# Differential attention's rotation and mixing: sums on GpSimd, coefficients for three tiles, another order of features

## The chip, the core and the metric

The kernel runs on one core of a Trainium2 chip. A core has five engines, each with its own stream of instructions, which it works through in order: TensorE (PE: matmuls, with weight loads shown apart as PEld), VectorE (DVE), ScalarE (ACT), GpSimd (POOL) and SyncE (SP, which here issues DMAs). They wait for each other through semaphores. SBUF and PSUM are the on-chip memories; PE writes to PSUM. The metric is the device time of one launch in microseconds; lower is better.

## The reference

Two post-norm layers, each a feed-forward half step, a token mixer, a cross-attention into 256 memory tokens, and a second feed-forward half step. Layer 0's mixer is the differential attention that this change touches; layer 1's is a pooling mixer. There are 512 tokens of 1024 features, all float32.

```python
q = rope(q.reshape(B, S, H, 2, dk), c5, s5)      # H = 8 heads, 2 components, dk = 64
k = rope(k.reshape(B, S, H, 2, dk), c5, s5)      # feature e is rotated with feature e + 32
lam = exp(sum(lq[0] * lk[0])) - exp(sum(lq[1] * lk[1])) + lam_init
s = einsum('bqhcd,bkhcd->bhcqk', qblk, k) * dk ** -0.5     # one score matrix per component
p = softmax(where(mask, s, min), axis=-1)
a = p[:, :, 0] - lam * p[:, :, 1]
o = einsum('bhqk,bkhe->bqhe', a, v)
o = o * rsqrt(mean(o ** 2) + eps) * subln_g * (1 - lam_init)
```

## The kernel before, in words

A float32 product is made of three matmuls: each operand is split into a high part (a cast, on ScalarE) and a low part (what the cast left out, a subtraction on VectorE), and high by high, low by high and high by low are summed in PSUM. `wh` and `wl` are the parts of weights, `qk` those of queries and keys, `a` those of mixed probabilities, `v` those of values.

`da_main` projects, head by head, query and key, and for every second head the values of two heads. `da_side` does the rest of a head: scores, softmax, mixing, the product with the values, the norm. `weave` writes the two into one program: after each piece of `da_main` it lets `da_side` go on, by estimated times, so that PE has projections to work on while a head's softmax runs on the other engines. A scheduler of the framework then fixes one order for each engine, and every engine keeps to its own at run time.

What the change and the prediction speak of, by the lines of the kernel before:

- `cols_rope` (L290, L293): splits one head's query or key weights, and puts the features of a head in an order that suits the rotation. The cast is one operation over 128 x 1024. The low part is two operations, one for each half of the features' quarters, over 128 x 512 each. There are 16 such weights.
- `da_rope` (L1129 to L1132): rotates a projected query or key. A shuffle on VectorE swaps the 16-partition halves of each group of 32 into `t2`; VectorE multiplies the projection by the cosines into `t1`; GpSimd multiplies `t2` by the sines; VectorE adds both. Then come the high part (ScalarE, L140 for a query, L135 for a key) and the low part (VectorE, L141 or L136). It runs 16 times.
- `da_scores` (L1162, L1171, L1174): PE's scores for the four tiles of 128 tokens, i = 0 to 3, tile i over the first (i + 1) x 128 keys and for both components. All six banks that PE and the other engines share here are taken for them, also the one into which the squares of the head before (L1220) are written. Then, on VectorE, mask and minimum (L1171), and on ScalarE the exponentials with their row sums (L1174).
- `da_mix` (L1187 to L1189): the reciprocal of the second component's row sum, the coefficient from it, and the mix, for one tile after another. It stands behind the masks of the head's last tile.
- `da_turn` (L506 with `pt<-ident,p`): PE transposes the mixed tile; `a` is its high and low part.
- `da_out` (L1210, L1211, L1216, L1217, L1220, then L1227 to L1230): PE's product with the values into `po`; for two tiles at a time a copy on ScalarE and a sum on VectorE into `o`; the squares on ScalarE; after the last tile four small operations on GpSimd that end with a power. `da_scale` uses the result.

The tiles `t1` and `t2` come from one pool of two buffers.

Of the kernel before, what the change touches and what calls it, by code (L numbers as in the profile page):

```python
# [9 lines left out]
F32 = mybir.dt.float32  # L10
# [3 lines left out]
ALU = mybir.AluOpType  # L14
# [3 lines left out]
P = 128  # L18
D = 1024
S = 512  # L20
NT = S // P
# [98 lines left out]
class Trunk:  # L120
# [163 lines left out]
    def cols_rope(self, raw, j, wait=False):  # L284

        nc = self.nc
        w = self.hl([P, 8, P])
        src = raw[:, j].rearrange("p k (m h q e) -> p (k m) q h e", m=2, h=2, q=2)
        hi, lo = (t.rearrange("p k (m q h e) -> p (k m) q h e", m=2, q=2, h=2) for t in w)
        nc.scalar.copy(hi, src)  # L290
        with self.tc.issue_after(self.turned[1].ins) if wait else nullcontext():
            for q in range(2):
                self.last_low = nc.vector.tensor_sub(  # L293
                    lo[:, :, q], src[:, :, q], hi[:, :, q].bitcast(F32)
                )
        return w

    def wide(self, raw):
# [827 lines left out]
    def da_rope(self, ps):  # L1126
        nc = self.nc
        t1, t2 = self.tmp("rt"), self.tmp("rt")
        nc.vector.stream_shuffle(t2, ps, [(i + 16) % 32 for i in range(32)])  # L1129
        nc.vector.tensor_tensor(t1, ps, self.ropeC, ALU.mult)  # L1130
        nc.gpsimd.tensor_tensor(t2, t2, self.ropeS, ALU.mult)
        nc.vector.tensor_tensor(t1, t1, t2, ALU.add)  # L1132
        return t1

    def da_query(self, ps):
# [11 lines left out]
    def da_scores(self, st, before):  # L1147

        nc = self.nc
        q, k, mm, terms = st["q"], st["k"], self.nc.tensor.matmul, ((0, 0), (1, 0), (0, 1))  # L1150
# [11 lines left out]
                    mm(banks[i][m], q[a][rows, qi], k[b][rows, kn], start=a == b, stop=b == 1)  # L1162
        for i in SC_ORDER:
            n = (i + 1) * P
            mx, rc, cf = self.small("mx"), self.small("rc", (P, 1)), self.small("cf", (P, 1))
            sm = st["sm"][:, i]
            p = [self.tmp("p")[:, :n] for m in range(2)]
            with self.tc.high_priority():
                for m in range(2):
# [10 lines left out]
            st["m", i] = p, sm, rc, cf  # L1180

    def da_mix(self, st, i):

        nc = self.nc
        p, sm, rc, cf = st.pop(("m", i))
        with self.tc.issue_after(st["masked"].ins):
            nc.vector.reciprocal(rc, sm[:, 1:2])  # L1187
            nc.vector.scalar_tensor_tensor(cf, sm[:, 0:1], self.nlam, rc, ALU.mult, ALU.mult)
            nc.vector.scalar_tensor_tensor(p[0], p[1], cf, p[0], ALU.mult, ALU.add)  # L1189
        st["p", i] = p[0]  # L1190

# [573 lines left out]
```

## Time and profile before

| what | value |
|---|---|
| device time, median of 3 runs | 1913.4 us (1912.26 to 1915.36) |
| span of the profiled execution | 1913.0 us, granted TensorE clock 0.999 |
| attention heads, as part of the span | about 355 to 560 us |
| PE busy in that stretch | 200.5 of 205.0 us |
| the rotation's sums on VectorE, L1132 | 16 of 682 ns, 10.9 us |
| the rotation's products on GpSimd, L1131 | 16 of 1289 ns, 20.6 us |
| low parts of query and key weights, L293 | 32 of 833 ns, 26.0 us |
| reciprocals and coefficients, L1187 and L1188 | 32 of 156 ns and 32 of 211 ns |

The span runs from the first to the last instruction of one execution that a profiler recorded; the device times are those of other executions, without it. In a row of the timeline stand the start in us from the span's begin, the duration in us, the engine, the line of the kernel, the operation, what it writes and reads, the sizes and a count. In brackets is the time for which the engine sat idle before, and what ended that. An instruction's record may overlap the next one's by some 0.08 us, since engines work in a pipeline. A row of waits gives the waiting engine and line, the one that it waited for, the sum in us, the number of times and the longest.

### The profile page before, as it was taken

The numbers are of one execution on the slowest core, as the hardware profiler recorded it, in microseconds if no ns is written. First come the engines' busy times: TensorE is split into PE (matmuls) and PEld (weight loads), VectorE is DVE, ScalarE is ACT, GpSimd is POOL, SyncE is SP. The second block draws the span as 40 slices with busy tenths as digits, with TensorE's granted clock in tenths as the row PEclk, the third lists the DMA queues.
The fourth block names the chain that finished last, engine by engine and source line by source line (L and its number), as shares of the span: only waits on it lengthen the run. The fifth ranks groups of instructions, "written<-read, shape, count | busy, mean of one in ns | idle before, by whom it ended". The sixth has DMA issues, their size and how long they took to land.

```text
span 1913.0 us, 32564 instructions
## 1 busy us (share of the span) xinstructions
PE 1894.9 (99%) x13136; PEld 1733.1 (91%) x13136; DVE 1550.6 (81%) x2250; ACT 1003.8 (52%) x1546; POOL 317.3 (17%) x274
## 2 busy tenths in 40 slices
PE   9999999999999999999999999999999999999998
PEld 8999998888878888999998999999899889999997
DVE  7888889888867558889888988898787568898886
ACT  6555554566645435645554655455455436555552
POOL 3112120111110001221220311212130012211210
PEclk9999999999999999999999999999999999999999
DMA  9978772323225327987785687878344438877861
GB/s 248 216 166 187 166 146 82 91 67 89 89 67 155 111 66 198 182 179 162 144 192 179 109 179 165 183 163 184 111 133 133 134 87 171 178 159 166 188 132 56
DMA packets 246743, 277.96 MB, mean 145 GB/s; under 512 B 8256, under 2 KB 212544, under 8 KB 246592
## 3 DMA queue, kind: packets, MB, share of 16 engines
q0 software_dynamic: 92928, 92.29, 31.5%
q1 hardware_dynamic: 153664, 183.59, 30.0%
q8 instruction: 103, 1.69, 0.4%
q14 instruction: 48, 0.39, 0.1%
HBM read 273.75 MB, written 2.10 MB: 144 GB/s over the span
## 4 chain that ended last, share of the span: by engine, by line
PE 85%; DVE 10%; ACT 2%; DMA 1%; issue 1%; POOL 1%; SPq 0%; DVEq 0%; ACTq 0%; POOLq 0%
PE x L221 7%; PE x L220 7%; PE x L222 7%; PE ps L220 4%; PE z L221 4%; PE z L220 4%; PE z L222 4%; PE ps L222 4%; PE ps L221 4%; PE px L222 2%; PE px L220 2%; PE px L221 2%; PE pt L506 2%; PE y L222 2%; PE x L757 2%; PE xq L222 2%
## 5 line engine op out<-in xcount | busy, mean ns | idle before, releaser
L725 POOL DMA_DIRECT2D ra<-in_ffn_w_in_dram x132 | 170.7, 1314 | 982.3 <-DVE wl L732 966.5
L730 ACT CAST wh<-ra 128x1024 fp32r<-128x1024 f32 x176 | 185.1, 1053 | 208.0 <-PE x L221 63.3
L732 DVE TENSOR_TENSOR wl<-ra,wh 128x1024 fp32r<-128x1024 f32 x176 | 214.4, 1223 | 66.5 <-ACT wh L730 66.1
L220 PE MATMUL x<-xe,wh 128*128 128x256 f32 x704 | 195.0, 277 | 0.0
L221 PE MATMUL x<-xe,wh 128*128 128x256 f32 x704 | 194.8, 277 | 0.0
L222 PE MATMUL x<-xe,wl 128*128 128x256 f32 x704 | 194.8, 277 | 0.0
L730 ACT CAST wh<-rc 128x1024 fp32r<-128x1024 f32 x132 | 139.0, 1053 | 102.4 <-PE x L221 41.6
L135 ACT CAST wh<-b 128x1024 fp32r<-128x1024 f32 x112 | 117.8, 1052 | 130.4 <-PE x L221 66.1
L732 DVE TENSOR_TENSOR wl<-rc,wh 128x1024 fp32r<-128x1024 f32 x132 | 160.3, 1222 | 25.5 <-ACT wh L730 25.5
L136 DVE TENSOR_TENSOR wl<-b,wh 128x1024 fp32r<-128x1024 f32 x112 | 136.9, 1222 | 41.0 <-ACT wh L135 41.0
L220 PE MATMUL x<-xh,wh 128*128 128x256 f32 x536 | 148.7, 277 | 0.0
L221 PE MATMUL x<-xl,wh 128*128 128x256 f32 x536 | 148.3, 277 | 0.0
L222 PE MATMUL x<-xh,wl 128*128 128x256 f32 x536 | 148.3, 277 | 0.0
L220 PEld LDWEIGHTS x<-xe,wh 128*128 128x128 f32 x704 | 132.4, 188 | 1.3
L221 PEld LDWEIGHTS x<-xe,wh 128*128 128x128 f32 x704 | 132.3, 188 | 1.3
L222 PEld LDWEIGHTS x<-xe,wl 128*128 128x128 f32 x704 | 132.2, 188 | 0.0
L136 DVE TENSOR_TENSOR wl<-raw,wh 128x1024 fp32r<-128x1024 f32 x64 | 82.4, 1296 | 41.1 <-ACT wh L135 40.5
L221 PEld LDWEIGHTS x<-xl,wh 128*128 128x128 f32 x536 | 100.8, 188 | 0.7
L220 PEld LDWEIGHTS x<-xh,wh 128*128 128x128 f32 x536 | 100.7, 188 | 0.7
L222 PEld LDWEIGHTS x<-xh,wl 128*128 128x128 f32 x536 | 100.6, 188 | 0.0
L135 ACT CAST wh<-raw 128x1024 fp32r<-128x1024 f32 x64 | 66.4, 1049 | 61.0 <-PE xq L221 19.1
L220 PE MATMUL z<-xe,wh 128*128 128x256 f32 x352 | 97.5, 277 | 0.0
(447 smaller groups left out, 6266.0 us busy)
## 6 DMA issues: line engine op xcount, KB each, us to landing
ra<-in_ffn_w_in_dram POOLq DMA_DIRECT2D x132, 512.0 KB, 7.0
rc<-in_ffn_w_in_dram SPq DMA_DIRECT2D x88, 512.0 KB, 5.8
b<-in_ffn_w_out_dram SPq DMA_DIRECT2D x76, 512.0 KB, 4.8
ra<-in_ffn_w_in_dram SPq DMA_DIRECT2D x44, 512.0 KB, 4.7
rc<-in_ffn_w_in_dram POOLq DMA_DIRECT2D x44, 512.0 KB, 7.8
raw<-in_xa_wkv_dram SPq DMA_DIRECT2D x16, 1024.0 KB, 5.4
raw<-in_da_w_qkv_dram SPq DMA_DIRECT2D x16, 512.0 KB, 5.2
raw<-in_xa_wq_dram SPq DMA_DIRECT2D x8, 1024.0 KB, 5.7
```

The source lines that it names most:

```text
L135: self.nc.scalar.copy(hi, src),
L136: self.nc.vector.tensor_sub(lo, src, hi.bitcast(F32)),
L220: self.first_mm = mm(out, w[0], x[0], start=start, stop=False, skip_group_check=again)
L221: mm(out, w[0], x[1], start=False, stop=False, skip_group_check=again)
L222: self.last_mm = mm(out, w[1], x[0], start=False, stop=stop, skip_group_check=again)
L506: self.turns = [self.nc.tensor.transpose(pt[:, j], b, self.ident) for j, b in enumerate(blocks)]
L725: nc.gpsimd.dma_start(t, source(*block), accum_op=ALU.add)
L730: hi = nc.scalar.copy(v[0], raw)
L732: lo = nc.vector.tensor_sub(v[1], raw, v[0].bitcast(F32))
L757: self.last_mm = nc.tensor.matmul(ps[:, j], v[i][:, k, j * P : (j + 1) * P], x[l][:, k], start=n == i == l == 0, stop=n == 7 and i == 1, s ...
```

## The change

It has three parts, all in the differential attention.

1. In `da_rope` the sum of `t1` and `t2` moves from VectorE to GpSimd, right behind GpSimd's product.
2. In `da_mix` the reciprocals and coefficients of tiles 0 to 2 are made by one operation each, over three columns, when tile 0 is mixed; tile 3 has its own.
3. In `cols_rope` the features of a component are paired by parity: feature 2r + q goes to place 32q + r, where before the places were made of runs of 16. Features e and e + 32 still come to lie 16 places apart in one group of 32, so the shuffle is the same, and the table of frequencies follows. The low part becomes one operation over 128 x 1024 that reads every second element, and so does the cast.

```diff
-    rope = np.stack([inv[quarter * 16 + e], np.where(half == 0, -1.0, 1.0)], axis=1).astype(np.float32)
+    rope = np.stack([inv[2 * e + quarter], np.where(half == 0, -1.0, 1.0)], axis=1).astype(np.float32)
...
-        src = raw[:, j].rearrange("p k (m h q e) -> p (k m) q h e", m=2, h=2, q=2)
-        hi, lo = (t.rearrange("p k (m q h e) -> p (k m) q h e", m=2, q=2, h=2) for t in w)
+        src = raw[:, j].rearrange("p k (m r q) -> p (k m) q r", m=2, q=2)
+        hi, lo = (t.rearrange("p k (m q r) -> p (k m) q r", m=2, q=2) for t in w)
         nc.scalar.copy(hi, src)
         with self.tc.issue_after(self.turned[1].ins) if wait else nullcontext():
-            for q in range(2):
-                self.last_low = nc.vector.tensor_sub(
-                    lo[:, :, q], src[:, :, q], hi[:, :, q].bitcast(F32)
-                )
+            self.last_low = nc.vector.tensor_sub(lo, src, hi.bitcast(F32))
...
         nc.gpsimd.tensor_tensor(t2, t2, self.ropeS, ALU.mult)
-        nc.vector.tensor_tensor(t1, t1, t2, ALU.add)
+        nc.gpsimd.tensor_tensor(t1, t1, t2, ALU.add)
...
-            mx, rc, cf = self.small("mx"), self.small("rc", (P, 1)), self.small("cf", (P, 1))
-            sm = st["sm"][:, i]
+            mx, sm = self.small("mx"), st["sm"][:, i]
...
-            nc.vector.reciprocal(rc, sm[:, 1:2])
-            nc.vector.scalar_tensor_tensor(cf, sm[:, 0:1], self.nlam, rc, ALU.mult, ALU.mult)
+            if i in (0, NT - 1):
+                n = slice(0, NT - 1) if i == 0 else slice(i, NT)
+                rc, st["cf"] = self.small("rc", (P, NT)), self.small("cf", (P, NT))
+                rc, cf, sm = rc[:, n], st["cf"][:, n], st["sm"][:, n]
+                nc.vector.reciprocal(rc, sm[:, :, 1])
+                nc.vector.scalar_tensor_tensor(cf, sm[:, :, 0], self.nlam, rc, ALU.mult, ALU.mult)
+            cf = st["cf"][:, i : i + 1]
             nc.vector.scalar_tensor_tensor(p[0], p[1], cf, p[0], ALU.mult, ALU.add)
```

The scheduler's orders change with it. Line numbers of the changed kernel are three lower in `da_rope`. On VectorE, from the product of head 2's query with the cosines to the shuffle of its key, before and now (`wl` here are low weights of values, `o` is the output's sum, `a` the low part of head 1's mixed tiles):

```order
L1130 TENSOR_TENSOR rt<-q,ropeC 128x512
L136 TENSOR_TENSOR wl<-raw,wh 128x1024
L136 TENSOR_TENSOR a<-pt,a 128x384
L1132 TENSOR_TENSOR rt<-rt 128x512
L1217 TENSOR_TENSOR o<-o,po 128x256
L141 SCALAR_TENSOR_TENSOR qk<-rt,qk 128x512
L136 TENSOR_TENSOR a<-pt,a 128x512
L1129 STREAM_SHUFFLE rt<-k 128x512
```

```order
L1127 TENSOR_TENSOR rt<-q,ropeC 128x512
L136 TENSOR_TENSOR wl<-raw,wh 128x1024
L136 TENSOR_TENSOR a<-pt,a 128x384
L141 SCALAR_TENSOR_TENSOR qk<-rt,qk 128x512
L1218 TENSOR_TENSOR o<-o,po 128x256
L136 TENSOR_TENSOR a<-pt,a 128x512
L1126 STREAM_SHUFFLE rt<-k 128x512
```

The sum is gone, and the query's low part now stands ahead of the output's sum and of a. On ScalarE the query's high part stands likewise ahead of the output's copy, the first square and the cast of a.

On GpSimd, from head 2's rotations (query, key) to that of head 3's query, before and now (`f` are the four small operations of head 1's norm, and the first two of head 2's):

```order
L1131 TENSOR_TENSOR rt<-rt,ropeS 128x512 x2
L1229 TENSOR_TENSOR f<-f,sq 128x4
L1230 TENSOR_TENSOR f<-f,mhalf 128x4
L1131 TENSOR_TENSOR rt<-rt,ropeS 128x512
L1227 TENSOR_SCALAR f<-sd 128x4
L1228 TENSOR_TENSOR f<-f,sd 128x4
```

```order
L1128 TENSOR_TENSOR rt<-rt,ropeS 128x512
L1129 TENSOR_TENSOR rt<-rt 128x512
L1128 TENSOR_TENSOR rt<-rt,ropeS 128x512
L1129 TENSOR_TENSOR rt<-rt 128x512
L1230 TENSOR_TENSOR f<-f,sq 128x4
L1231 TENSOR_TENSOR f<-f,mhalf 128x4
L1128 TENSOR_TENSOR rt<-rt,ropeS 128x512
L1129 TENSOR_TENSOR rt<-rt 128x512
L1228 TENSOR_SCALAR f<-sd 128x4
L1229 TENSOR_TENSOR f<-f,sd 128x4
```

Each product has its sum right behind it; the two rows of the norm stand, as before, ahead of head 3's product.

On VectorE, from the key's product with the cosines at head 2 to the masks of head 2 (`q` is head 3's query), before and now:

```order
L1130 TENSOR_TENSOR rt<-k,ropeC 128x512
L293 TENSOR_TENSOR wl<-raw,wh 128x16x32
L1132 TENSOR_TENSOR rt<-rt 128x512
L1217 TENSOR_TENSOR o<-o,po 128x256
L293 TENSOR_TENSOR wl<-raw,wh 128x16x32
L136 TENSOR_TENSOR qk<-rt,qk 128x512
L1129 STREAM_SHUFFLE rt<-q 128x512
L1130 TENSOR_TENSOR rt<-q,ropeC 128x512
L293 TENSOR_TENSOR wl<-raw,wh 128x16x32
L1132 TENSOR_TENSOR rt<-rt 128x512
L293 TENSOR_TENSOR wl<-raw,wh 128x16x32
L141 SCALAR_TENSOR_TENSOR qk<-rt,qk 128x512
```

```order
L1127 TENSOR_TENSOR rt<-k,ropeC 128x512
L292 TENSOR_TENSOR wl<-raw,wh 128x1024
L136 TENSOR_TENSOR qk<-rt,qk 128x512
L1218 TENSOR_TENSOR o<-o,po 128x256
L1126 STREAM_SHUFFLE rt<-q 128x512
L1127 TENSOR_TENSOR rt<-q,ropeC 128x512
L292 TENSOR_TENSOR wl<-raw,wh 128x1024
L141 SCALAR_TENSOR_TENSOR qk<-rt,qk 128x512
L1167 ISA p,mx<-sc,mask 128x128
```

The masks of head 2 stand behind the low part of head 3's query, before and now; the output's sum has come behind the key's low part.

More of the change, by code (lines that the diff above doesn't have):

```diff
@@ L1179, in da_scores @@
                         self.da_scale(before)
-            st["m", i] = p, sm, rc, cf
+            st["m", i] = p
     def da_mix(self, st, i):
         nc = self.nc
-        p, sm, rc, cf = st.pop(("m", i))
+        p = st.pop(("m", i))
         with self.tc.issue_after(st["masked"].ins):
-            nc.vector.reciprocal(rc, sm[:, 1:2])
-            nc.vector.scalar_tensor_tensor(cf, sm[:, 0:1], self.nlam, rc, ALU.mult, ALU.mult)
+            if i in (0, NT - 1):
[5 more added lines that the diff above has]
+            cf = st["cf"][:, i : i + 1]
             nc.vector.scalar_tensor_tensor(p[0], p[1], cf, p[0], ALU.mult, ALU.add)
```

## The prediction

> **What bounds the kernel now.** I read the page's busy shares first.
>
> ```profile
> PE 1894.9 (99%) x13136; PEld 1733.1 (91%) x13136; DVE 1550.6 (81%) x2250; ACT 1003.8 (52%) x1546; POOL 317.3 (17%) x274
> ```
>
> TensorE (PE) is busy 99% of the span, so an edit moves the end only by the time for which PE itself waits. The change touches the attention heads alone, from about 355 to 560 us; the table of waits for that stretch (first two lines) and for the rest (last line, PE's longest there) says what there is.
>
> ```profile
> PEld pt L506 <- DVE p L1189: 5.5, 5, 1.7
> PEld sc L1162 <- ACT po L1220: 0.9, 3, 0.4
> PE pk L222 <- DVE wl L136: 0.6, 2, 0.5
> ```
>
> Five times PE waits for a mixed tile before it transposes it (L506), 5.5 us in all: the most that the change can win. After 560 us PE hardly waits, so nothing there absorbs a shift: what the heads gain or lose reaches the end whole. Next, the timeline at the masks of head 2, where such a wait stands.
>
> ```profile
> 414.12 1.04 POOL L1230 TENSOR_TENSOR f<-f,mhalf 128x4 f32<-128x4 f32 x1
> 415.56 0.75 DVE L1129 STREAM_SHUFFLE rt<-q 128x512 f32<-128x512 f32 x1
> 416.38 1.29 POOL L1131 TENSOR_TENSOR rt<-rt,ropeS 128x512 f32<-128x512 f32 x1 [1.21 <-DVE rt L1129]
> 416.79 1.43 DVE L293 TENSOR_TENSOR wl<-raw,wh 128x512 fp32r<-128x512 f32 x1
> 418.14 0.68 DVE L1132 TENSOR_TENSOR rt<-rt 128x512 f32<-128x512 f32 x1
> 418.86 0.63 ACT L140 ACTIVATE qk<-rt 128x512 fp32r<-128x512 f32 x1 [2.49 <-DVE rt L1132]
> 419.52 0.69 DVE L141 SCALAR_TENSOR_TENSOR qk<-rt,qk 128x512 fp32r<-128x512 f32 x1
> 420.13 0.28 DVE L1171 CUSTOM_DVE_ANT_0 p<-sc,mask 128x128 f32<-128x128 f32 x1
> 423.42 0.30 DVE L1187 RECIPROCAL rc<-sd 128x1 f32<-128x1 f32 x3
> 423.88 0.74 DVE L1189 SCALAR_TENSOR_TENSOR p<-p,cf 128x128 f32<-128x128 f32 x2
> 424.28 0.33 PE L506 MATMUL pt<-ident,p 128*128 128x128 f32 x1 [0.87 <-DVE p L1189]
> ```
>
> This is head 3's query rotation, and head 2's masks (L1171) stand behind its last step (L141) on VectorE (DVE). So the rotation's length sets the masks of the head before, its mix, and PE's first transpose. That is the path to price.
>
> **Who has the port.** The L293 row took 1.43 us where the same row on an idle GpSimd (POOL) takes 0.68: it ended 0.55 us after GpSimd's product (416.38 + 1.29 = 417.67). What happens when both engines queue up shows in the pooling stage:
>
> ```profile
> 1397.81 1.29 POOL L1355 TENSOR_TENSOR X<-X,p 128x512 f32<-128x512 f32 x1 [4.94 <-DVE xl L136]
> 1407.90 2.06 DVE L136 TENSOR_TENSOR wl<-raw,wh 128x1024 fp32r<-128x1024 f32 x1 [0.18 <-ACT wh L135]
> 1408.85 2.26 POOL L1355 TENSOR_TENSOR X<-X,p 128x512 f32<-128x512 f32 x1
> 1409.89 2.30 DVE L136 TENSOR_TENSOR wl<-raw,wh 128x1024 fp32r<-128x1024 f32 x1
> 438.92 1.04 POOL L1230 TENSOR_TENSOR f<-f,mhalf 128x4 f32<-128x4 f32 x1
> 439.47 1.30 DVE L293 TENSOR_TENSOR wl<-raw,wh 128x512 fp32r<-128x512 f32 x2 [1.84 <-ACT wh L290]
> ```
>
> A GpSimd sum of this very shape (L1355) takes 1.29 alone. Behind another of its kind, with a VectorE operation of two SBUF inputs waiting (the low weights at 1407.90), it takes 2.26: VectorE gets the port between the two, and the next low operation waits in turn. They alternate. A low operation over 1024 ends 1.08 us after GpSimd lets go (1409.89 + 2.30 = 1412.19 against 1408.85 + 2.26 = 1411.11), and a sum that waited ends 1.14 us after the low operation (1411.11 against 1407.90 + 2.06 = 1409.96). The last two rows say that GpSimd's power over four columns does not hold VectorE up: two half operations in 1.30 beside it.
>
> **The change part by part.** *Coefficients.* Three reciprocals at 0.07 and the coefficients at 0.13 each stood before the first mix (423.42 to 423.88, 0.46); one of each over three columns makes about 0.33, as it waits for the third tile's exponentials, which the third reciprocal did too. So 0.13 earlier per head. Head 0's third tile is also mixed before the key's rotation.
>
> *Low weights.* One operation over 1024 in place of two over 512. Between the bounds 1.22 (contiguous, as 1.08 + 0.14 above) and twice that (each element of the read with step two costing two) I take 1.22: the old form, with broken runs, cost 0.65 per 512, like a contiguous row. By the Trainium skill (SBUF — State Buffer, the note on cachelines under Door 1: The DMA port swizzle) a step of up to four fp32 reads at full rate; that would give the same 1.22, and no row here reads with step two.
>
> *The sum.* From the end E of GpSimd's product, the sum was over at E + 1.15 (418.82): half a low operation, then 0.68. Now the whole low operation gets the port at E, ends at E + 1.08, and GpSimd's sum at E + 2.23: 1.07 later. If GpSimd kept the port it would end at E + 1.27, but the low operation at E + 2.35, and L141 stands behind it: 0.4 later instead. The rows above alternate, so I take 1.07. The 16 sums leave VectorE (16 of 0.68, 11 us), but that time lay beside PE's projections; where VectorE sat waiting before and after the sum is what counts.
>
> *What queues behind it.* ScalarE and VectorE now have L140 and L141 ahead of the output's copy, sum and squares, which used to go first. Head 2's query shows the price:
>
> ```profile
> 402.59 0.74 DVE L1129 STREAM_SHUFFLE rt<-q 128x512 f32<-128x512 f32 x1
> 404.47 1.32 DVE L136 TENSOR_TENSOR wl<-raw,wh 128x1024 fp32r<-128x1024 f32 x1
> 406.77 0.41 DVE L1217 TENSOR_TENSOR o<-o,po 128x256 f32<-128x256 f32 x1
> 406.88 0.63 ACT L140 ACTIVATE qk<-rt 128x512 fp32r<-128x512 f32 x1 [1.44 <-DVE rt L1132]
> 407.42 0.27 ACT L1220 ACTIVATE po<-o 128x128 f32<-128x128 f32 x1
> 407.71 0.57 ACT L135 CAST a<-pt 128x512 fp32r<-128x512 f32 x1
> 408.31 0.69 DVE L136 TENSOR_TENSOR a<-pt,a 128x512 fp32r<-128x512 f32 x1
> 409.66 0.22 PE L1211 MATMUL po<-v,a 128*128 128x128 f32 x1
> 413.37 0.28 ACT L1220 ACTIVATE po<-o 128x128 f32<-128x128 f32 x1
> 413.85 0.20 POOL L1229 TENSOR_TENSOR f<-f,sq 128x4 f32<-128x4 f32 x1 [2.62 <-ACT po L1220]
> ```
>
> GpSimd's sum ends at 405.79 + 1.14 = 406.93; L140 starts at 406.96, L141 0.67 later at 407.63, the output's sum at 408.23 (was 406.77), the square at 408.67, the cast of a at 408.96, its low part from 409.56 to 410.25. PE needs that at 409.66 and a weight load of 0.19 ahead: **0.8 us of new wait, head 1**.
>
> From there the key: shuffle at 410.17, product from 410.99 to 412.28, low operation to 413.36, sum to 414.50, L141 from 415.20, output's sum to 416.21, squares to 417.08 (was 413.77), then on GpSimd the f row and the power to 418.5. Head 3's query product stands behind these in GpSimd's queue, so it comes not at 416.38 but after 418.5; the low operation, whose cast was behind the squares, has the port from 418.08 to 419.22, the product ends at 420.44, the sum at 421.7, L141 at 422.4, the masks at 423.0 in place of 420.13. The transpose comes 2.85 - 0.13 = 2.7 us late, of which PE has waited 0.8: **1.9 more, head 2**. The same steps for head 4's query and key (its shuffle at 449.75, GpSimd's sum over at 454.1, L141 from 454.8, a's low part over at 457.4 and loaded by 457.6 against 456.73 below; then the squares at 464.2, the power to 465.6, masks 2.9 late) give **0.9 at head 3 and 1.9 at head 4**.
>
> The other places, with their rows:
>
> ```profile
> 377.54 0.33 PE L506 MATMUL pt<-ident,p 128*128 128x128 f32 x1 [0.21 <-DVE p L1189]
> 381.75 0.55 PE L506 MATMUL pt<-ident,p 128*128 128x128 f32 x3 [0.61 <-DVE p L1189]
> 384.73 0.60 PE L506 MATMUL pt<-ident,p 128*128 128x128 f32 x4
> 456.73 0.22 PE L1211 MATMUL po<-v,a 128*128 128x128 f32 x1
> 485.89 1.74 PEld L1162 LDWEIGHTS sc<-qk 64*128 64x128 f32 x24 [0.36 <-ACT po L1220]
> 492.06 1.29 POOL L1131 TENSOR_TENSOR rt<-rt,ropeS 128x512 f32<-128x512 f32 x1
> 494.66 0.33 PE L506 MATMUL pt<-ident,p 128*128 128x128 f32 x1 [1.26 <-DVE p L1189]
> 505.23 0.22 PE L1211 MATMUL po<-v,a 128*128 128x128 f32 x1
> 509.77 0.52 PEld L1162 LDWEIGHTS sc<-qk 64*128 64x128 f32 x5 [0.19 <-ACT po L1220]
> ```
>
> - Head 0: masks 1.4 late (1.07, and 0.3 from the key before it), less 0.13: +1.3 at 377.54. The wait at 381.75 goes, since the third mix no longer follows the key's rotation: -0.8. The fourth mix now stands behind the key's longer chain (sum at 383.9, L141 at 384.6, mix from 385.3 to 386.1) where PE wants it at 384.73 + 0.5: +0.9. Together **+1.4**.
> - Head 5: its scores wait for the squares, which move behind L141 by 0.6: **+0.6** at 485.89. Its mixes no longer wait for the key's sum, but they, and the coefficients, have two SBUF inputs and meet GpSimd's product (to 493.35) and sum (to 494.65): first transpose at about 495.2, **+0.5** at 494.66. If coefficients of three columns pass while GpSimd works, the first mix comes between product and sum, at 493.35, and PE waits at the second tile instead, for 0.2 less than now in all. The wide operations above all waited, so I take +0.5. By the Trainium skill (SBUF — State Buffer, SBUF: two separate sides) the lock is for every VectorE operation with two SBUF inputs against a GpSimd one that reads SBUF, which would give the same; no narrow one met GpSimd's wide product here.
> - Heads 5 and 6: the cast of a behind L140 as at head 1, low part at 506.4 against 505.23 + 0.5: **+0.8**. Then the key's chain ends with squares at 513.2 (were done by 509.72), and the scores that reuse their bank move from 509.77 to 513.3, 3.7 late with 1.35 paid: **+2.3**.
>
> Sum: 1.4 + 0.8 + 1.9 + 0.9 + 1.9 + 0.6 + 0.5 + 0.8 + 2.3 = 11.1 us on the span of 1913.0, that is 1924.1; the median of the runs lies 0.4 above that span, so **1924.5**. With the port kept by GpSimd the same walk gives +7.5, with every place a third dearer about +15: its own range is 1920 to 1929.
>
> **The rivals.** *The sum is hidden.* If GpSimd's sum ran right behind its product and the low operation cost nobody time, the chain would be 0.2 longer per query, the coefficients would pay 0.13 back, 0.8 and 1.0 of head 0's and 5's waits would go, and the new order would still cost some 0.5 at heads 1 and 3: 1912.5, no change. For it: GpSimd is 17% busy. Against it: the alternation at 1408.85. *VectorE relieved.* It loses 11 us of sums and some of the low and small operations. If all five waits at L506 came of VectorE's load, they would go: 1913.4 - 5.5 = 1908. Against it: at 415.56 to 420.13 VectorE stands in one chain, not in a backlog. It is decided by whether L141 starts earlier than E + 1.85. *Step two is dear.* If the low operation took 2.3 us, it would add 1.07 at some seven of the places above: 1932. For it: no row shows such a read.
>
> **How the numbers follow.** My forecast 0.68, hidden 0.14, relieved 0.09, dear 0.09. About 0.2% (3.8 us) is what a measurement of this kernel tells from no change, so the same is 1909.6 to 1917.2. Faster gets the relieved case and a little of the hidden one, 0.1; the same gets the rest of the hidden one and a tail of the forecast in which half the places have slack that I missed, 0.17; slower 0.73. The range from 1914 to 1931 leaves out 0.09 + 0.05 below and 0.06 above.
>
> **What would show it.** Right: low operations right behind GpSimd's product, and sums of about 2.2 us; the masks of heads 2 and 4 some 2.9 us later against PE's clock of matmuls; waits of PE at L506 that grow to 2 us and more; the power ahead of a late product. Wrong: sums of 1.3 us, L141 less than 2 us after E, or low operations well over 1.3 us on a free port.

## The result, and the profile after

The changed kernel took 1929.76 us in the median of four runs (1929.33 to 1930.07), the kernel before 1912.83 beside it: a ratio of 1.0089, with an interval of 1.0076 to 1.0102. It is slower by 16.9 us, on the side of the forecast. The time lies 5.3 us beyond the forecast's number (1924.5), inside the range given for all cases (1914 to 1931), and 0.8 us outside the mechanism's own range (1920 to 1929). The profiled execution of the changed kernel took 1930.0 us and has a span of 1928.2. Two executions that took several times as long, one of the kernel before (5290 us) and one of the last filler kernel below (9063 us), are left out of the ratios.

The busy shares of the changed kernel look like those of before:

```profile
PE 1899.5 (99%) x13136; PEld 1735.9 (90%) x13136; DVE 1543.2 (80%) x2186; ACT 1004.0 (52%) x1546; POOL 348.9 (18%) x290
```

PE's busy time grew by 4.6 us for the same 13136 matmuls, which is a first sign that waits are not the whole cost. VectorE lost 7 us and GpSimd gained 32. Ahead of the heads the profiles differ by 2 us, after them by less than 1. From the first query's shuffle to the first mask of head 7 the heads cost 16.5 us more, about the difference of the medians.

The table of waits of the changed kernel for the heads (waiting engine and line, the one waited for, sum in us, times, longest; `PEld` counts the idle time before a weight load, `PE` that before the matmul itself):

```profile
PEld pt L503 <- DVE p L1190: 13.3, 5, 3.9
...
PE pt L503 <- DVE p L1190: 11.6, 5, 3.4
...
PEld sc L1159 <- ACT po L1221: 3.5, 4, 2.5
...
PE sc L1159 <- ACT po L1221: 2.1, 1, 2.1
...
PEld po L1212 <- DVE a L136: 1.4, 3, 0.5
```

The five waits before transposes grew from 5.5 to 13.3 us on PE's weight loads (from 3.8 to 11.6 on its matmuls), and a new one of 2.1 stands before head 6's scores. From here on a wait of PE is its idle time before the matmul. The key rotation of head 2 shows where they begin, in the timeline of the changed kernel:

```profile
411.12 1.29 POOL L1128 TENSOR_TENSOR rt<-rt,ropeS 128x512 f32<-128x512 f32 x1 [4.17 <-DVE rt L1126]
411.46 2.04 DVE L292 TENSOR_TENSOR wl<-raw,wh 128x1024 fp32r<-128x1024 f32 x1
412.50 2.16 POOL L1129 TENSOR_TENSOR rt<-rt 128x512 f32<-128x512 f32 x1
414.69 0.62 ACT L135 CAST qk<-rt 128x512 fp32r<-128x512 f32 x1 [3.79 <-POOL rt L1129]
415.34 0.69 DVE L136 TENSOR_TENSOR qk<-rt,qk 128x512 fp32r<-128x512 f32 x1 [1.84 <-ACT qk L135]
415.95 0.41 DVE L1218 TENSOR_TENSOR o<-o,po 128x256 f32<-128x256 f32 x1
```

GpSimd's product ends at 412.41. The low operation, which had waited for the port, ends at 413.50, 1.09 later; the sum, in GpSimd's queue since 412.50, ends at 414.66, which is 2.25 behind the product. VectorE then sits idle for 1.84 us until the high part is there. Over the heads the sum took 1.92 us on average:

```profile
L1129 POOL TENSOR_TENSOR rt<-rt 128x512 f32<-128x512 f32 x16 | 30.7, 1921 | 1.3
```

Head 3's query and the masks of head 2 follow in the same timeline, the place that the prediction showed of before:

```profile
416.39 0.73 DVE L1126 STREAM_SHUFFLE rt<-q 128x512 f32<-128x512 f32 x1
...
417.59 1.04 POOL L1231 TENSOR_TENSOR f<-f,mhalf 128x4 f32<-128x4 f32 x1
...
418.28 1.23 DVE L292 TENSOR_TENSOR wl<-raw,wh 128x1024 fp32r<-128x1024 f32 x1 [0.59 <-ACT wh L290]
418.60 2.05 POOL L1128 TENSOR_TENSOR rt<-rt,ropeS 128x512 f32<-128x512 f32 x1
...
420.73 1.29 POOL L1129 TENSOR_TENSOR rt<-rt 128x512 f32<-128x512 f32 x1
...
422.05 0.63 ACT L140 ACTIVATE qk<-rt 128x512 fp32r<-128x512 f32 x1 [3.80 <-POOL rt L1129]
...
422.71 0.69 DVE L141 SCALAR_TENSOR_TENSOR qk<-rt,qk 128x512 fp32r<-128x512 f32 x1 [3.20 <-ACT qk L140]
...
423.32 0.28 DVE L1167 CUSTOM_DVE_ANT_0 p<-sc,mask 128x128 f32<-128x128 f32 x1
...
426.00 0.68 DVE L1167 CUSTOM_DVE_ANT_0 p<-sc,mask 128x512 f32<-128x512 f32 x1
...
426.52 0.19 ACT L1170 ACTIVATION_READ_ACCUMULATOR p<-p,mx 128x1 f32 x1
...
426.74 0.18 DVE L1187 RECIPROCAL rc<-sd 128x3 f32<-128x3 f32 x1
426.95 0.22 DVE L1188 SCALAR_TENSOR_TENSOR cf<-sd,nlam,rc 128x3 f32<-128x3 f32 x1
427.21 1.28 DVE L1190 SCALAR_TENSOR_TENSOR p<-p,cf 128x128 f32<-128x128 f32 x3
...
427.61 0.33 PE L503 MATMUL pt<-ident,p 128*128 128x128 f32 x1 [3.37 <-DVE p L1190]
```

The power stands ahead of the query's product, and the low operation has the port first: on a free port it takes 1.23 although it reads every second element. From shuffle to masks pass 6.93 us where 4.57 did. PE waits 3.37 us where it waited 0.87.

What no wait shows is in the granted clock. Rows of stretches of the changed kernel follow: busy us of PE, PEld, DVE, ACT and POOL with their counts, then the granted TensorE clock, the share of the DMA engines and GB/s.

```profile
373.35:376.76 3.41, 1.98 (x12) 1.54 (x10) 3.32 (x16) 3.41 (x13) 0.00 (x0) 1.00 0.00 0
...
424.54:427.95 3.41, 0.34 (x3) 0.34 (x4) 3.29 (x13) 3.41 (x12) 0.37 (x2) 1.00 0.00 0
427.95:431.37 3.42, 3.42 (x18) 3.42 (x18) 3.38 (x10) 2.81 (x9) 1.81 (x3) 0.50 0.00 0
475.74:479.15 3.41, 0.61 (x3) 0.18 (x1) 3.33 (x18) 3.35 (x13) 0.00 (x0) 1.00 0.08 32
479.15:482.57 3.42, 2.80 (x7) 2.15 (x8) 3.35 (x11) 3.39 (x10) 1.30 (x3) 0.50 0.00 0
520.11:523.53 3.42, 1.35 (x10) 0.67 (x8) 2.72 (x13) 2.53 (x11) 0.69 (x3) 1.00 0.53 206
523.53:526.94 3.41, 3.41 (x16) 3.25 (x16) 2.77 (x11) 3.41 (x12) 0.98 (x3) 0.50 0.00 0
```

Three times in the heads the clock was 0.50 for 3.413 us; the kernel before has no such stretch there. They lie whole multiples of 3.413 apart (51.2 and 44.4 us), and ahead of each stands one window of that length in which PE was busy for 0.34, 0.61 and 1.35 us, that is idle for 3.07, 2.80 and 2.07. The first row above is another window of the same grid, with head 0's wait in it: idle for 1.43, and the clock stayed. PE does half as much in such a stretch, so it costs up to 1.7 us: about 1.7 + 1.4 + 1.7 = 4.8 here (in the second one PE was busy for 2.80 only). The two traces show the loss directly as well. PE runs the same matmuls in both kernels, and the changed kernel's, set beside those of the kernel before, fall behind by 1.55, 1.22 and 1.48 us within the three stretches and never catch up: 4.25 us, somewhat less than the 4.8. New waits of 11.8 us (added up place by place further down) and these stretches make 16.1 to 16.6, against 16.5 measured.

### The profile page after: what moved, and what is told of

The parts are those of the page before. It is cut to its first block, busy times and chain, and to the rows that moved or that the text cites. A ratio compares the mean times of both kernels' runs of the same rounds, so it can differ in the third digit from the quotient of the medians.

```text
span 1928.2 us, 32512 instructions
## 1 busy us (share of the span) xinstructions
PE 1899.5 (99%) x13136; PEld 1735.9 (90%) x13136; DVE 1543.2 (80%) x2186; ACT 1004.0 (52%) x1546; POOL 348.9 (18%) x290
## 4 chain that ended last, share of the span: by engine, by line
PE 80%; DVE 10%; ACT 4%; POOL 2%; DMA 2%; issue 1%; SPq 0%; DVEq 0%; ACTq 0%; POOLq 0%
PE x L220 7%; PE x L221 7%; PE x L222 7%; PE z L220 4%; PE z L222 4%; PE z L221 4%; PE ps L220 4%; PE ps L222 4%; PE ps L221 4%; PE px L222 2%; PE px L220 2%; PE px L221 2%; PE y L222 2%; PE xq L220 2%; PE xq L222 2%; PE xq L221 2%
## 5 line engine op out<-in xcount | busy, mean ns | idle before, releaser
L136 DVE TENSOR_TENSOR wl<-b,wh 128x1024 fp32r<-128x1024 f32 x112 | 136.7, 1220 | 40.2 <-ACT wh L135 40.2
L136 DVE TENSOR_TENSOR wl<-raw,wh 128x1024 fp32r<-128x1024 f32 x64 | 84.2, 1326 | 41.4 <-ACT wh L135 40.8
```

Source lines behind the costliest of these rows:

```text
L136: self.nc.vector.tensor_sub(lo, src, hi.bitcast(F32)),
```

## The experiments

The first theory: the sum on GpSimd makes the rotation longer, since the two engines alternate on the port, and everything else follows from that, the order and the clock included. Rivals: the new order of the queues, the coefficients or the read with step two cost as much by themselves; or PE's lower clock is no cost of its own, because PE only meets its next wait earlier. Four kernels took the change apart.

**The sum back on VectorE**, all else as changed:

```diff
-        nc.gpsimd.tensor_tensor(t1, t1, t2, ALU.add)
+        nc.vector.tensor_tensor(t1, t1, t2, ALU.add)
```

> The changed kernel with the rotation's sum back on VectorE; the wide low operation and the three-column coefficients stay. My theory (the sum on GpSimd, which waits for the port behind the low operation, makes most of the 16.9 us): the low operation now stands ahead of the sum on VectorE, which is over at E + 1.8 (E is the end of GpSimd's product), against E + 2.2 in the changed kernel and E + 1.15 before; TensorE's waits of 3.7 us at heads 2 and 4 fall to about 2, and the three stretches of half clock go. 1914.5 to 1918. Rival (the low operation or the coefficients make the loss): it stays above 1924.

1914.67 us, ratio 1.0011 (1.0002 to 1.0020). Its waits before the transposes, in the table for the heads:

```profile
PE pt L503 <- DVE p L1190: 5.2, 4, 1.6
```

No stretch of half clock is left in the heads. So the sum's place carries 15 of the 17 us, and its two companions together cost some 2.

**The sum alone**, the other edit in the kernel before, whose low operations are two halves:

```diff
-        nc.vector.tensor_tensor(t1, t1, t2, ALU.add)
+        nc.gpsimd.tensor_tensor(t1, t1, t2, ALU.add)
```

> The kernel before with one edit alone: the rotation's sum on GpSimd. The low operations are still halves of 512. My theory (the port alternates): the first half ends at E + 0.55, GpSimd's sum at E + 1.7, 0.5 later than before and 0.5 earlier than in the changed kernel; the new order of the queues (high parts of the rotation ahead of the output's copy and squares) comes with it. Sum of about 5 to 9 us: 1918 to 1922, and above that if a wait is long enough to halve the clock. Rival (GpSimd's sum is hidden and the loss comes from the other two edits): 1912 to 1914. Rival (GpSimd keeps waiting for both halves): sums of 2.2 us and 1925 or more.

1925.83 us, ratio 1.0070 (1.0055 to 1.0085). The key rotation of head 2 in its timeline:

```profile
409.66 1.29 POOL L1131 TENSOR_TENSOR rt<-rt,ropeS 128x512 f32<-128x512 f32 x1 [4.16 <-DVE rt L1129]
...
410.00 3.19 DVE L293 TENSOR_TENSOR wl<-raw,wh 128x512 fp32r<-128x512 f32 x2
...
411.02 1.61 POOL L1132 TENSOR_TENSOR rt<-rt 128x512 f32<-128x512 f32 x1
```

A half operation goes between product and sum in place of a whole one; it ends 0.55 us after the product, the whole one 1.09. The sum takes 1.61 instead of 2.16: the hold scales with the operation that waits. Two stretches of half clock stand here, behind windows with these rows:

```profile
471.87:475.28 3.41, 0.98 (x5) 0.46 (x3) 3.41 (x19) 3.41 (x14) 0.00 (x0) 1.00 0.36 138
...
516.25:519.66 3.41, 1.33 (x9) 0.84 (x9) 3.19 (x15) 2.56 (x13) 1.15 (x2) 1.00 0.11 43
```

At heads 2 and 4 PE waits for 2.41 and 2.43 us. Head 4's wait fell whole into one window, and the clock halved; head 2's fell on two windows, 1.30 and 1.11, and it did not. That is the same wait with and without the loss. The second window is the one before head 6's scores, idle for 2.08. Both stretches were full of matmuls, which makes up to 3.4 us, and with them the run lies above the 1918 to 1922 that the waits alone gave.

**The coefficients alone**, the sum and the features as before:

```diff
+            if i in (0, NT - 1):
+                n = slice(0, NT - 1) if i == 0 else slice(i, NT)
...
+            cf = st["cf"][:, i : i + 1]
```

> The kernel before with one edit alone: mixing coefficients of three tiles at once. My theory: the first mix of a head comes 0.14 us later after its masks (0.53 against 0.39 us in the two profiles) where the prediction had it 0.13 earlier, which costs some 0.14 at heads 0, 2 and 4; head 0's second wait (0.8) goes, since the third mix no longer stands behind the key's rotation. 1912 to 1914, no change. Rival (the coefficients are what made heads 2 and 4 dear): 1916 or more.

1911.69 us, ratio 0.9994 (0.9984 to 1.0003): no change.

**The parity and the one low operation alone**:

```diff
-            for q in range(2):
-                self.last_low = nc.vector.tensor_sub(
-                    lo[:, :, q], src[:, :, q], hi[:, :, q].bitcast(F32)
-                )
+            self.last_low = nc.vector.tensor_sub(lo, src, hi.bitcast(F32))
```

> The kernel before with one edit alone: features paired by parity and one low operation over 1024. My theory: on a free port it takes 1.23 us as in the changed kernel; ahead of the sum it makes the sum end at E + 1.8 instead of E + 1.15, so the masks of heads 0, 2 and 4 come about 0.6 later, and head 5's first mix as well: 2 to 3 us in all, 1914.5 to 1917. Rival (step two is dear or the wide operation is the main cause): 1920 or more, with low operations above 1.5 us on a free port.

1914.69 us, ratio 1.0011 (1.0001 to 1.0021). Where the low operation fills the gap, VectorE's own sum stands behind a whole one instead of a half and ends 3.85 us after the shuffle's start instead of 3.32 (head 1's query). Of the change's parts one costs nothing, one some 2 us and one 13.4 (1.0070 of 1912.6). That is a little less than the 16.9 of all three together; the whole low operation lengthens the sum on GpSimd more than a half does, which fits, but no run prices this by itself.

**What holds the port.** In the changed kernel the low operation became a scaling with one input (a constant instead of the high part is its second operand, so the low weights are not the remainder). If only operations with two SBUF inputs hold the port, GpSimd's sum should run free:

```diff
-            self.last_low = nc.vector.tensor_sub(lo, src, hi.bitcast(F32))
+            self.last_low = nc.vector.tensor_scalar(lo, src, 2.0**-13, None, ALU.mult)
```

> The changed kernel with the low operation of the heads' query and key weights replaced by one of the same 1024 elements with a single SBUF input (the weights scaled, so the low weights no longer hold the remainder: this part of the computation is changed). It stays where it is in the queue, between GpSimd's product and sum; the values' low operations keep two inputs. The sum stays on GpSimd. My theory (two-input operations of VectorE and GpSimd exclude each other, and this makes the rotation late): sums of 1.3 us, the rotation's low part starts at 4.25 from the shuffle (5.1 in the changed kernel, 4.0 before) wherever such an operation stands in the gap, and it takes no time on VectorE that was not free. The waits at heads 2 and 4 fall to 1.4 to 2.0 and the half clocks go, but for head 6: 1914 to 1920. Rival (GpSimd's slower sum and the hand-over to ScalarE are the cost, or any VectorE operation blocks): sums stay at 2.2, 1925 or more.

1921.96 us, ratio 1.0052 (1.0037 to 1.0068): above what was expected. Head 2's key in its timeline:

```profile
408.34 1.29 POOL L1128 TENSOR_TENSOR rt<-rt,ropeS 128x512 f32<-128x512 f32 x1 [4.16 <-DVE rt L1126]
...
408.69 1.49 DVE L292 TENSOR_SCALAR wl<-raw 128x1024 fp32r<-128x1024 f32 x1
...
409.71 1.62 POOL L1129 TENSOR_TENSOR rt<-rt 128x512 f32<-128x512 f32 x1
```

The scaling waits for GpSimd too: it ends 0.55 us after the product, where 0.69 is its whole time on a free port, and the sum is held up with it, to 1.62 us. So the port is not a matter of two inputs alone. The experiment still supports the mechanism: the hold between product and sum halved (1.09 to 0.55), the sum ends 1.70 behind the product instead of 2.25, and the ratio fell from 1.0089 to 1.0052. The profiled execution has no stretch of half clock in the heads, but it was the quickest of the four (1918.94 us, mean granted clock 0.999). The others had a mean clock of 0.996 to 0.998 and took 1921.26 to 1923.49, so that half clock seems to have come and gone here from one execution to the next; no trace of the other three shows where. The Trainium skill (SBUF — State Buffer, Who interferes with whom) names one-input VectorE operations in a mode with two ports among those that hold the pair; the 0.69 for 1024 elements, a little more than half of the subtraction's 1.23, and the row above agree.

**The order of the queues.** In the changed kernel ScalarE and VectorE keep the order of before at four rotations: the output's copy and sum, or the parts of a, go first (`queue_behind` is a helper of the kernel that keeps the order of two instructions of one engine):

```diff
+        for h, rot, out in ((2, 0, (1, 1)), (2, 1, (1, 3)), (7, 0, ("a", 5, 3)), (7, 1, (5, 3))):
+            for turn, first in zip(self.heads[h][1]["rot"][rot], self.outs[out]):
+                self.queue_behind(turn, first)
```

> The changed kernel with the queues of ScalarE and VectorE put back to the order of before at the four places where they changed places: head 2's query and key behind head 1's copies and sums of the output, head 7's query behind head 5's last cast, head 7's key behind its copy and sum. GpSimd's sum and the wide low operation stay. My theory (what stands behind the late rotation in the queues is part of the loss): the waits for head 1's last tile (0.6) and head 6's scores (2.15) go, head 2's falls by about 1, and one or two of the three half-clock stretches with them: 1921 to 1925. Rival (the order does not matter, the length of the rotation alone does): 1927.5 to 1930.5.

1923.41 us, ratio 1.0058 (1.0044 to 1.0071). The new waits at head 1's values and before head 6's scores are gone, and head 2's wait fell from 3.37 to 2.09 us; head 4's, which was not touched, stayed (3.42 and 3.35), with its half clock, the only one left in the profile. GpSimd's rows at head 2 and at head 4:

```profile
415.54 1.04 POOL L1235 TENSOR_TENSOR f<-f,mhalf 128x4 f32<-128x4 f32 x1
416.71 1.29 POOL L1130 TENSOR_TENSOR rt<-rt,ropeS 128x512 f32<-128x512 f32 x1
...
466.35 1.04 POOL L1235 TENSOR_TENSOR f<-f,mhalf 128x4 f32<-128x4 f32 x1
467.36 2.05 POOL L1130 TENSOR_TENSOR rt<-rt,ropeS 128x512 f32<-128x512 f32 x1
```

At head 2 the power is done in time and the product follows its shuffle by 0.83, as it does elsewhere; at head 4 the late power holds the product up and the low operation gets ahead of it. The order of these four rotations is thus worth about a third of the loss (1.0089 against 1.0058), and the prediction's walk had it. But it is the sum that moved it: in the run with the sum back on VectorE, the output's sum stands ahead of L141 at head 2's query again, and the two companions cost 2 us in all.

**The clock.** Is the half clock a cost beside the waits? Idle matmuls (matmuls whose results are not used) fill PE's time before the three long waits, so that its work begins as late as before but PE is not idle meanwhile:

```diff
+        if i == 0 and st["h"] in (2, 4):
+            self.fill(bank, 10)
...
+            if i == NT - 1 and st["h"] == 6:
+                for _ in range(14):
+                    mm(one[0][:, 2 * P :], x[:, :P], x[:, : 2 * P], start=True, stop=True)
```

> The changed kernel with idle matmuls in front of the three longest waits of TensorE: ten of 128x512 (0.23 us each) ahead of the first transpose of heads 2 and 4, fourteen of 128x256 (0.12 us each) ahead of the last scores of head 6. Their results are overwritten or never read. They are over before the wait ends, so no work starts earlier; only the array is busy meanwhile. My theory (a stretch of 3.41 us in which the array idled for 2 us or more is followed by 3.41 us at half clock): the three half-clock stretches go and with them 1.7 + 1.4 + 1.7 = 4.8 us: 1924 to 1926. Rival (the half clock has another cause, or the extra time is in the waits alone): 1929 to 1931, with the three stretches still there.

1933.65 us, ratio 1.0109 (1.0095 to 1.0122): slower still, a miss. The three stretches were gone, but the fillers had also moved the scheduler's order on ScalarE: the casts of a at heads 2 and 4 stood behind the key's rotation, with waits that the changed kernel does not have.

```profile
PE po L1223 <- ACT a L135: 4.0, 2, 2.0
```

Two other waits had got half clock instead, behind windows with 1.87 and 2.06 us of idle time. It decides nothing, since two things had changed.

The second try pins those orders:

```diff
+        for h, low in ((2, LOWS[0]), (4, LOWS[1])):
+            self.queue_behind(self.lows[low][0], self.outs["a", h, 0][0])
+            self.queue_behind(self.lows[low][1], self.outs["a", h, 1][1])
+            self.queue_behind(self.outs["mix", h, 3], self.outs["a", h, 0][1])
...
```

> The idle matmuls again, with the queues of ScalarE and VectorE pinned to the changed kernel's order behind them (in the first form the casts of head 2's and 4's first transposed tiles had moved behind the key's rotation, a new wait of 2.2 us each). My theory (half clock is a cost of its own): no half clock behind the three waits, 1.7 + 1.4 + 1.7 us less in this profile than with it; other waits may still bring one. 1924.5 to 1927. Rival (behind heads 2 and 4 TensorE only runs into the next wait on VectorE's chain, so the half clock there was covered, and only head 6's counts): 1927.5 to 1929.

1926.95 us, ratio 1.0077 (1.0063 to 1.0090); the interval overlaps that of the changed kernel. In the profiles, mask of head 2 to mask of head 3 now cost 0.15 us more than in the kernel before, against 1.70 in the changed kernel, heads 4 to 5 0.12 against 1.37, heads 6 to 7 1.01 against 2.50. But head 5's window, idle for 1.96, had got a stretch of its own. So a last kernel fills there too, with three more orders pinned:

```diff
+FILL = {2: 10, 4: 10, 5: 3}
...
-        if i == 0 and st["h"] in (2, 4):
-            self.fill(bank, 10)
+        if i == 0 and st["h"] in FILL:
+            self.fill(bank, FILL[st["h"]])
```

> The idle matmuls a third time: at the three waits of the second form and three more of 128x512 ahead of head 5's first transpose, where the second form had its one half-clock stretch; queues pinned to the changed kernel's order. My theory (a half-clock stretch follows wherever the array idled for some 2 of 3.41 us, and is a cost of its own of up to 1.7 us): none at heads 2, 4, 5 and 6; the heads then cost what the waits alone make, about 11.8 us against before: 1923.5 to 1925.5, and 1.7 more in executions where head 0's wait of 2.0 us falls into one stretch. Rival (TensorE only meets the next wait earlier): 1927 to 1930, as the second form or the changed kernel.

1924.65 us in the median of five runs (1923.35 to 1926.41), ratio 1.0061 (1.0048 to 1.0075), which lies just below the changed kernel's 1.0076 to 1.0102. The mean granted clock of the five is 0.998 to 0.999, that of the changed kernel's four 0.995 to 0.996. Its sums on GpSimd are those of the changed kernel (1.92 us on average); only PE is not idle in the waits. The heads of its profile cost 4.3 us less, and its ratio is 0.0028 lower, which is 5 us: about what the three stretches were reckoned to cost. Together with the matmuls that fall behind inside the stretches, this shows the half clock as a cost of its own. One stretch is left, at head 0:

```profile
373.28:376.69 3.41, 1.52 (x11) 1.23 (x10) 3.29 (x14) 3.41 (x12) 0.30 (x2) 1.00 0.00 0
376.69:380.10 3.41, 3.41 (x18) 3.41 (x17) 3.41 (x8) 1.80 (x5) 2.12 (x3) 0.50 0.02 5
```

Head 0's wait is that of the changed kernel, whose window had 1.43 idle; here the grid lies so that one window has 1.89, and the clock halves. PE's wait for the fourth mix, 0.98 us in the changed kernel, took up most of what that stretch cost.

**Versions that might win.** If the low operation is moved out of the gap between product and sum, GpSimd's sum should run at 1.29:

```diff
+        for late, first in (
+            (m["v", 2][0], ("rot", 0, 0)), (m["v", 2][1], ("rot", 0, 0)), (low[4], ("rot", 0, 1)),
...
+            self.queue_behind(late, m[first])
```

> The changed kernel with the low operations moved out from between product and sum, on VectorE: behind the rotation's own low part, or behind the last mix of the head. GpSimd's sum then finds the port free and should take 1.3 us instead of 2.15, over at E + 1.35 against E + 2.2 (before: E + 1.15). My theory (the port between product and sum is what makes the rotation late, and the order of the queues follows from it): waits at heads 2 and 4 of 1.4 to 1.9, no half clock, 1913 to 1918. Rival (the hand-over to GpSimd and back, or GpSimd's slow sum itself, is the cost): 1921 or more.

1926.08 us, ratio 1.0072 (1.0058 to 1.0085): a miss. Head 0's query in its timeline:

```profile
357.59 1.28 POOL L1134 TENSOR_TENSOR rt<-rt 128x512 f32<-128x512 f32 x1
...
359.57 0.69 DVE L141 SCALAR_TENSOR_TENSOR qk<-rt,qk 128x512 fp32r<-128x512 f32 x1 [2.85 <-ACT qk L140]
360.19 2.35 DVE L136 TENSOR_TENSOR wl<-raw,wh 128x1024 fp32r<-128x1024 f32 x2
...
362.46 0.73 DVE L1131 STREAM_SHUFFLE rt<-k 128x512 f32<-128x512 f32 x1
```

The sum is free, and the query's low part begins 4.16 us behind the shuffle, where it is 5.36 in the changed kernel. But VectorE now idles for 2.85 us in the gap and does the two low operations behind it, ahead of the key's shuffle, which comes 7.05 behind the query's; in the kernel before it is 5.60. The waits of heads 0, 2 and 4 are 2.38, 2.86 and 2.89 us, with two stretches of half clock. The interval overlaps that of the changed kernel: the later key took back most or all of what the shorter sum gave.

The same move with the sum on VectorE and the coefficients of before (parity and one low operation alone, low operations behind the rotation), shown against the changed kernel:

```diff
-        nc.gpsimd.tensor_tensor(t1, t1, t2, ALU.add)
+        nc.vector.tensor_tensor(t1, t1, t2, ALU.add)
...
+            self.queue_behind(late, m[first])
```

> A version meant to beat both: the kernel before with the parity pairing and its one low operation (coefficients per tile, sum on VectorE), and the low operations moved out from between product and sum as in the run beside it. The sum then follows GpSimd's product at once, over at E + 0.7 against E + 1.15 before. My theory: each of the five waits ahead of a transpose shrinks by up to 0.45, 2 us in all: 1909.5 to 1912. Rival (the low operation only moves to a place where it holds up as much): 1912 to 1915.

1912.08 us in the median of eleven runs, ratio 0.9999 (0.9990 to 1.0008). The sum ends 0.7 us behind the product instead of 1.15, and PE's waits at the transposes fell to 3.3 us from 3.8, but the time is that of the kernel before.

Last, the two halves of before, one of them between the sum and L141, where VectorE waits for ScalarE anyway, the other behind, with the coefficients of three columns:

```diff
+        for j, r in ((4, 1), (5, 2), (6, 3), (8, 5), (9, 6), (10, 7), (13, 8), (14, 9), (15, 10)):
+            self.queue_behind(low[j][0], self.adds[r])
+            self.queue_behind(m["rot", r // 2, r % 2], low[j][0])
```

> A second version meant to beat both: the kernel before with the three-column coefficients, low operations in halves, and the halves moved: one into the gap between the sum and the rotation's low part, where VectorE waits 0.7 us for ScalarE, the other behind the rotation; sum on VectorE. The sum then stands right behind GpSimd's product (E + 0.7 against E + 1.15), and no more than 0.65 us of low work is put behind the rotation. My theory: head 0's second wait (0.8) goes, the waits at heads 2, 4 and 5 shrink by 0.3 to 0.4 each: 1909.5 to 1911.5. Rival (the half behind the rotation holds up as much as it gave): 1911.5 to 1914.

1911.06 us in the median of eleven runs, ratio 0.9994 (0.9986 to 1.0003). The waits at the transposes are down to 2.6 us, and the time cannot be told from that of the kernel before. No version found beats it measurably; all that could be won at the transposes were PE's 3.8 us of waits (5.5 counted on its weight loads).

## Why the prediction came out as it did

**Right: the mechanism and its size.** The low operation ends 1.09 behind the product and the sum 2.25; 1.08 and 2.23 were forecast. The low operation costs 1.23 on a free port; 1.22 was taken. The power stands ahead of the late product at head 2. PE's time from start to start of its matmuls at each place, less the same in the kernel before, stands against the forecast thus (it can differ by some 0.2 us from the idle time):

| place | forecast | measured |
|---|---|---|
| head 0: first transpose, second and fourth mix | +1.4 | +1.7 − 0.8 + 1.15 = +2.05 |
| head 1, values | +0.8 | +0.6 |
| head 2, first transpose | +1.9 | +2.5 |
| head 3, values | +0.9 | +1.0 |
| head 4, first transpose | +1.9 | +2.5 |
| head 5, scores | +0.6 | 0.0 |
| head 5, first transpose | +0.5 | +0.7 |
| head 5, last tile's values | +0.8 | +0.3 |
| head 6, scores | +2.3 | +2.15 |
| sum | 11.1 | 11.8 |

That the sums lie within 0.7 us of each other is in part luck: some places came out 2.15 us dearer than forecast, others 1.45 us cheaper.

**Wrong: the sum of waits was taken for the whole.** The step that failed is the one that carried the waits to the end as they are ("what the heads gain or lose reaches the end whole"). They do, and on top of that three of them halved PE's clock behind them, for 4.3 to 4.8 us. With the 0.7 us by which the waits were undersized, that makes up the 5.3 us by which the forecast fell short. The clock's row of before gave no hint, since no wait of the kernel before is long enough: PE's longest at these transposes is 1.26 us. The matmuls that fall behind within the stretches, and the last filler kernel, show that it is a cost of its own.

**Wrong in sign: the coefficients.** They were to bring the first mix 0.13 earlier, with 0.33 from the first reciprocal to the mix instead of 0.46. It is 0.47 (426.74 to 427.21): two steps that depend on each other cost 0.21 and 0.26, so that one of each over three columns takes as long as three of each over one column, which overlap. And the reciprocal starts 0.06 behind the end of the last mask (426.68), when the third tile's sums are there (426.71); before, the first of the three started ahead of that end, and the mix came 0.39 behind it instead of 0.53. So it is 0.14 later, 0.27 against the forecast, at heads 0, 2 and 4: nearly half of what these were undersized by.

**Wrong: head 5's scores.** The query's parts were to move ahead of the squares there, as at other heads; at this place the order did not change, and the idle time before the weight load is 0.36 in both kernels. Head 5's last tile was milder than head 1, whose steps it copied. The mixes of head 5 met GpSimd as assumed; the narrow coefficients were held up as well:

```profile
501.68 1.29 POOL L1128 TENSOR_TENSOR rt<-rt,ropeS 128x512 f32<-128x512 f32 x1
...
503.04 1.26 POOL L1129 TENSOR_TENSOR rt<-rt 128x512 f32<-128x512 f32 x1
```

```profile
501.86 0.17 DVE L1187 RECIPROCAL rc<-sd 128x1 f32<-128x1 f32 x1 [0.15 <-ACT p L1170]
501.94 1.17 DVE L1188 SCALAR_TENSOR_TENSOR cf<-sd,nlam,rc 128x3 f32<-128x3 f32 x2
503.03 2.34 DVE L1190 SCALAR_TENSOR_TENSOR p<-p,cf 128x128 f32<-128x128 f32 x3
```

(The first rows are GpSimd's, the others VectorE's, of the changed kernel.) Two coefficients that take 0.22 each elsewhere end only at 503.11, behind the product; the mixes behind them end behind the sum. The reciprocal, with one input, ran beside the product in 0.17.

**The rivals.** *The sum is hidden* fell with sums of 1.92 us. *VectorE relieved* fell with the idle times of 1.84 and 3.20 us in the rows above: the work taken from VectorE was replaced by waiting, and the rotation's low part (L141, L136) starts 2.06 to 3.77 us behind GpSimd's product, at ten of the sixteen 2.9, where the line to decide it was 1.85. *Step two is dear* fell with the 1.23 at 418.28; its number of 1932 came nearest to the time for another reason.

## What to carry to other kernels

Before moving an operation to an engine that is mostly idle, look at what stands ready on the other side of the shared port at that moment: an idle share of 83% did not help, since an operation of VectorE that was already waiting went between GpSimd's product and its sum, and its length was added to the chain. Moving such work out of the gap in which an engine waits anyway need not help either: it lands elsewhere on the same engine, and in the three versions here it took back most or all of what the shorter chain gave. When an edit lengthens waits of TensorE to some 2 us, price the clock too: the waits are then not the whole cost, and what comes on top depends on where they fall.

## What the runs showed of the hardware that was not expected

*The half clock.* In the traces of the seven kernels with such a stretch in the heads (the changed one, the sum alone, the order, the low operations behind, and the three with fillers), cut into windows of 3.413 us on each one's grid, all 12 windows in which PE was idle, by the profile's records, for 1.87 us or more (up to 3.07) were followed by a stretch at half clock, and none with 1.80 or less was. Each stretch lasted one window. A wait of 2.4 us may thus cost nothing more or up to 1.7 us, by its place on the grid. The Trainium skill (TensorE: Matmul & The Clock Gate, Part 1: The HAM clock gate) states a free-running window of 3413 ns and half rate after an idle one; length and rate agree. Its table under Why this matters for your kernels asks for no gaps of more than about 3 us; here a window idle for little more than half was enough, so that by this rule alone the wait of 2.07 us before head 6's scores would have passed as harmless.

*The port.* A one-input operation over 1024 elements that takes 0.69 us on a free port waits for GpSimd and holds it up, as the scaling showed. Narrow operations with two inputs wait as well: a coefficient over three columns, 0.22 us elsewhere, stood until a product of GpSimd was over, while a narrow reciprocal with one input did not wait.
